# Convolution and experts of a one-layer trunk: the inverse's last step respread over groups, and two matmuls of the expert projections merged into one

## The chip, the cores and the metric

The kernel runs on one core of a Trainium2 chip. The metric is device time in microseconds (us). The engines are TensorE (PE for matmuls, PEld for its weight loads), VectorE (DVE), ScalarE (ACT), GpSimd (POOL) and SyncE (SP); each works through its own queue in order. Transfers are issued by SP, POOL and ACT and carried by 16 shared DMA engines.

## The reference, cut to what matters

One layer over 2048 tokens of width 1024: adaLN, a Hyena mixer, a residual norm, and a mixture of 16 experts, each of which takes the 256 tokens that score highest for it.

```python
v, x1, x2 = jnp.split(u, 3, -1)                    # u: input projection and a 3-tap convolution
def long_conv(zin, o):
    y = irfft(rfft(zin, n=2 * L) * kf[o], n=2 * L)[:L]
    return y + zin * f_bias[o]
z = x1 * long_conv(v, 0)
z = x2 * long_conv(z, 1)
...
he = silu(xe @ w1) * (xe @ w3)                      # xe: the 256 tokens of an expert
ye = (he @ w2) * gate                               # added into the tokens' rows
```

All is float32. Where the kernel wants more speed than a float32 matmul it writes a number as a sum of two fp32r parts, high and low, and sums three products: high·high, high·low, low·high. `mm3` (lines 174 to 177) issues these three.

## The kernel before, in words

**Convolution** (`phase_conv`, about 1037 to 1606 us of the trace). The FFT is done as matmuls in steps. There are 8 jobs (`jobs`): four blocks of 256 channels for the first long convolution (jobs 0 to 3), then four for the second (4 to 7). A job has 16 groups `gp`, so the loop over `order` has 128 turns. What a turn does is written out by hand, and the order in the code is the order on every engine. A turn of group n holds:

- `fetch_k` and `fetch`: every second turn, 512 KB of filter spectra (`kr`) and of signal (`xr`), issued on SP up to nine turns ahead;
- `spec`, three turns ahead: two float32 matmuls on the filter into a bank `xp`, and four half-height ACT copies from it into `k`, the last one (line 832) with the sign turned;
- `fwd`, two turns ahead: two matmuls on the signal into `xp`, then four DVE operations that make the complex product `pz`;
- `inv`: two matmuls from `pz` into the one bank `ap`, an ACT copy into one of three tiles `ao`, and one turn later (`LAG`) two POOL-issued transfers of 128 KB that scatter `ao` into `bn` (`put`). An `ao` is free again when its transfers have landed.

When a job's 16 groups lie in `bn`, the inverse's last step takes eight pieces q, during the next job: `bst` (at gp 2 to 9, one a turn) multiplies a piece of `bn` into a bank `sb`; one turn later `gate` multiplies by `x` on DVE. In the first convolution `bsplit` first makes high and low parts of pieces 3 to 7 (two ACT casts, two POOL subtractions, one turn ahead), `gate` also splits its result (one ACT cast, one POOL subtraction), and `s1st` (at gp 4 to 11) starts the next convolution's forward step: for each of two halves th three fp32r matmuls of 512 columns into `sb`, an ACT copy into `s1t`, a POOL-issued store to `z1d`. In the second convolution `gate`'s result is stored to `zd` from POOL. `fetch_x` loads `x` two pieces at a time at gp 0, 2, 4, 6. The eight PSUM banks are four `xp`, three `sb`, one `ap`.

**Experts** (`phase_moe`, about 1915 to 4170 us). Per expert there are 16 turns (8 slices `fc` of the hidden width, 2 halves i). `project` writes one bank `ab` of two halves of 256 columns, one for w1 and one for w3: for each of them eight k-steps of `mm3` with 256 token columns. `flush` then issues the previous turn's `back`: 12 fp32r matmuls of 512 columns into four banks `acc`. `hidden` is a chain ACT silu, DVE product (line 1487), ACT cast `hh`, DVE subtraction `hl`; its result is read by `back` one turn later. Besides, each slice's weights are split (line 1380 an ACT cast, line 1381 a DVE subtraction, 128x2048 each, three times a slice), and `route` gathers and transposes the next expert's tokens into `xh` and `xl`, through two banks `tp`. For the first 13 experts a planner orders the instructions from its own cost estimates, in the order of the code where several are ready; the last three experts have an order written by hand.

Of the kernel before, what the change touches and what calls it, by code (L numbers as in the profile page):

```python
# [12 lines left out]
F32 = mybir.dt.float32  # L13
# [756 lines left out]
def phase_conv(tc, A, wst, s2, am, fud, ud, x1d, x2d, z1d, zd, O, after):  # L770
# [5 lines left out]
    with ExitStack() as st:  # L776
# [21 lines left out]

        def s1st(j, q):
            zh, zl = zs.pop((j, q))  # L800
            for th in range(2):
                p = ps.tile([128, 2, 256], F32, name="sb", bufs=3)
                mm3(nc, p, s1h[:, th], s1l[:, th], zh, zl)
                t = rt.tile([128, 2, 256], F32, name="s1t", bufs=3)
                nc.scalar.copy(t, p)
                nc.gpsimd.dma_start(z1d[jobs[j][0], th].rearrange("g (s n) c -> (g s) n c", s=8)[:, 2 * q:2 * q + 2], t)

# [14 lines left out]
        def spec(j, gp):  # L822

            r = kr.pop((j, gp))
            p = ps.tile([128, 2, 256], F32, name="xp", bufs=4)
            for i in range(2):
                nc.tensor.matmul(p[:, i], lhsT=s2[:, 2 * gp + i], rhs=r[:, i], start=True, stop=True)  # L827
            k = rt.tile([128, 2, 2, 256], F32, name="k", bufs=3)
            nc.scalar.copy(k[0:64, 0], p[0:64])
            nc.scalar.copy(k[64:128, 0], p[0:64])  # L830
            nc.scalar.copy(k[64:128, 1], p[64:128])
            nc.scalar.activation(k[0:64, 1], p[64:128], AF.Copy, scale=-1.0)
            if gp == 0:
                nc.vector.tensor_copy(k[64:65, 0, 0], k[64:65, 1, 0])
                nc.vector.memset(k[0:1, 1, 0], 0.0)
                nc.vector.memset(k[64:65, 1, 0], 0.0)
            kk[j, gp] = k
# [3 lines left out]
        def fwd(j, gp):  # L841
# [15 lines left out]
        def inv(j, gp):  # L857
# [8 lines left out]
            ao = wk.tile([128, 2, 256], F32, name="ao", bufs=3)  # L866
            nc.scalar.copy(ao, p)
# [31 lines left out]
        def bst(j, q):  # L899
            p = ps.tile([128, 2, 256], F32, name="sb", bufs=3)  # L900
            if jobs[j][1] == 0:
# [13 lines left out]
        def gate(j, q, p):  # L915
# [18 lines left out]
        order = [(j, gp) for j in range(8) for gp in range(16)]  # L934

        def ahead(n):
# [7 lines left out]
        for n, (j, gp) in enumerate(order):  # L944
            if j > 0 and gp % 2 == 0 and 0 <= gp < 8:
                fetch_x(j - 1, gp - 0)
            while bps:
                gate(*bps.pop(0))
            ahead(n)
            if 4 <= gp < 9 and j > 0:  # L950
                bsplit(j - 1, gp - 1)
            if 2 <= gp < 10 and j > 0:
                bst(j - 1, gp - 2)
            q = gp - 4
            if (j + 3, q) in zs:
                s1st(j + 3, q)
            inv(j, gp)
# [27 lines left out]
        def first(q):  # L985
            tag = ("xp", "sb")[q % 2] if q < 7 else "ap"
            halves.append(ps.tile([128, 2, 256], F32, name=tag, bufs={"xp": 4, "sb": 3, "ap": 1}[tag]))
            nc.tensor.matmul(halves[q], lhsT=zero[:, 0:128], rhs=zero, start=True, stop=False)
            last(q, 0)
# [430 lines left out]
def phase_moe(tc, A, rowd, ident, ones_f, lg, R, xnd, accd, out):  # L1420
    nc = tc.nc
    tab, lo, hi, slot, spf = R.tab, R.lo, R.hi, R.slot, R.spf
    with ExitStack() as st:
# [7 lines left out]
        def route(e):  # L1431
# [4 lines left out]
            yield  # L1436
            p = ps.tile([128, 2, 33], F32, name="tp")
            idx = wk.tile([128, 2], I32, name="idx", bufs=4)
# [15 lines left out]
            yield  # L1454
            xh = wk.tile([128, 8, 256], F32R, name="xh")
            xl = wk.tile([128, 8, 256], F32R, name="xl")
            nxt[:] = [idx, gate, xh, xl]
            for q in range(4):
                p = ps.tile([128, 2, 256], F32, name="tp")
# [4 lines left out]
                nc.scalar.copy(xh[:, 2 * q:2 * q + 2], p)  # L1464
                nc.vector.tensor_tensor(xl[:, 2 * q:2 * q + 2], p, f_(xh[:, 2 * q:2 * q + 2]), OP.subtract)
                yield
# [6 lines left out]

        def project(i, x, ws):

            xh, xl = x
            fs = slice(i * 128, i * 128 + 128)
            p = ps.tile([128, 2, 256], F32, name="ab")
            for j in range(2):
                for k in range(8):  # L1480
                    mm3(nc, p[:, j], ws[2 * j][:, k, fs], ws[2 * j + 1][:, k, fs], xh[:, k], xl[:, k], start=(k == 0), stop=(k == 7))
            return p

        def hidden(p):
            s = wk.tile([128, 256], F32, name="s")
            nc.scalar.activation(s, p[:, 0], AF.Silu)  # L1486
            nc.vector.tensor_tensor(s, s, p[:, 1], OP.mult)  # L1487
            hh = wk.tile([128, 256], F32R, name="hh")
# [22 lines left out]

        def settle(name, idx=None):


            x = wk.tile([128, 2, 1024], F32, name=name)
            if idx is None:
# [48 lines left out]
        for e in range(NE - 3):  # L1565
            idx, gate, *x = nxt
            acc = [[pa.tile([128, 512], F32, name=f"acc{h}{q}") for q in range(2)] for h in range(2)]
# [18 lines left out]
        with tc.manual_schedule():  # L1586
# [4 lines left out]
            for e in range(NE - 3, NE):  # L1591
                prev = acc, idx, gate
                idx, gate, *x = nxt
                acc = [[pa.tile([128, 512], F32, name=f"acc{h}{q}") for q in range(2)] for h in range(2)]
                rt = iter(()) if e == NE - 1 else route(e + 1)
                for n in range(16):
                    fc, i = divmod(n, 2)
                    if i == 0:
                        ws, nw = nw, []
                    p = project(i, x, ws)  # L1600
                    flush()
# [14 lines left out]
                    if todo:  # L1616
                        act.append(settle(todo[-2:], prev[1] if todo[0] == "-" else None))
                        next(act[-1])
# [10 lines left out]
            flush()  # L1629
            ys = [wk.tile([128, 1024], F32, name=n) for n in ("xh", "xl")]  # L1630

# [131 lines left out]
```

## Time and profile before

| | |
|---|---|
| time, median of 3 runs | 4176.95 us (4176.51 to 4177.35) |
| the profiled execution: its own time, and its span | 4177.93 us, 4176.1 us |
| mean granted TensorE clock | 0.971 |
| busy: PE, PEld, DVE, ACT, POOL | 93%, 80%, 63%, 45%, 26% of the span |
| DMA | 832.14 MB, 199 GB/s mean |

The span runs from the first to the last instruction; the execution has 1.8 us around it. Busy shares are means over stages with different limits, so the rows below are taken per stage. A matmul's duration in the trace is longer than the distance to the next one, because matmuls are pipelined; what one costs is the distance between starts.

### The profile page before, as it was taken

How to read it: one execution, taken by the hardware profiler on the slowest of the kernel's cores; microseconds unless marked ns; L12 is line 12 of the kernel's file. 1: busy time of each engine (PE TensorE's matmuls, PEld its weight loads, DVE VectorE, ACT ScalarE, POOL GpSimd, SP SyncE). 2: the span in 40 equal slices, each digit the busy share in tenths (PEclk: the TensorE clock that was granted, in tenths of full speed). 3: DMA queues.
4: the chain of work that ended last, by engine and by line, in shares of the span. 5: the costliest groups of instructions: out<-in, count | busy, mean ns of one | idle time of the engine just before them, and what ended most of it. 6: DMA issues, size and time to landing. Idle time of an engine off the chain costs nothing.

```text
span 4176.1 us, 59155 instructions
## 1 busy us (share of the span) xinstructions
PE 3898.9 (93%) x23158; PEld 3350.6 (80%) x23158; DVE 2639.2 (63%) x3636; ACT 1885.7 (45%) x2609; POOL 1067.4 (26%) x1106
## 2 busy tenths in 40 slices
PE   6788999999989998956999999999999999999997
PEld 2445787877767786746999999999999999998996
DVE  6997454776877786885555555555555555556666
ACT  4554332333888772122444444444444444444443
POOL 4674221221566542130000000000000000005635
PEclk7999999999999999977999999999999999999999
DMA  6565355666998996453656665666566656656664
GB/s 190 184 210 177 119 163 170 204 205 207 256 257 230 262 281 204 162 176 108 202 193 210 192 202 193 208 193 203 192 208 193 203 193 203 200 170 226 231 229 166
DMA packets 645843, 832.14 MB, mean 199 GB/s; under 512 B 56883, under 2 KB 532803, under 8 KB 643260
## 3 DMA queue, kind: packets, MB, share of 16 engines
q1 hardware_dynamic: 576066, 678.56, 50.9%
q0 software_dynamic: 52512, 146.97, 12.1%
q10 hardware_dynamic: 16986, 2.83, 0.4%
q8 instruction: 182, 2.98, 0.3%
q14 instruction: 97, 0.79, 0.1%
HBM read 643.82 MB, written 150.75 MB: 190 GB/s over the span
## 4 chain that ended last, share of the span: by engine, by line
PE 74%; DVE 8%; DMA 7%; POOL 4%; issue 3%; ACT 2%; SPq 0%; ACTq 0%; POOLq 0%; DVEq 0%
PE ab L175 11%; PE ab L177 11%; PE ab L176 11%; PE acc L175 5%; PE acc L176 5%; PE acc L177 5%; PE ip L175 4%; PE ip L177 4%; PE ip L176 4%; DMA bn<-ao 4%; PE op L175 1%; PE op L177 1%; PE op L176 1%; PE xp L827 1%; PE ap L865 1%
## 5 line engine op out<-in xcount | busy, mean ns | idle before, releaser
L177 PE MATMUL ab<-xh,w1l 128*128 128x256 f32 x2048 | 581.4, 284 | 3.1 <-DVE w1l L1381 2.9
L175 PE MATMUL ab<-xh,w1h 128*128 128x256 f32 x2048 | 582.8, 285 | 0.0
L177 PE MATMUL ab<-xh,w3l 128*128 128x256 f32 x2048 | 579.7, 283 | 0.5 <-DVE w3l L1381 0.5
L176 PE MATMUL ab<-xl,w1h 128*128 128x256 f32 x2048 | 579.8, 283 | 0.0
L176 PE MATMUL ab<-xl,w3h 128*128 128x256 f32 x2048 | 579.6, 283 | 0.0
L175 PE MATMUL ab<-xh,w3h 128*128 128x256 f32 x2048 | 579.6, 283 | 0.0
L1381 DVE TENSOR_TENSOR w2l<-w2r,w2h 128x2048 fp32r<-128x2048 f32 x126 | 297.5, 2361 | 316.9 <-ACT w2h L1380 316.9
L175 PE MATMUL acc<-w2h,hh 128*128 128x512 f32 x1024 | 404.3, 395 | 13.4 <-ACT hh L170 13.4
L176 PE MATMUL acc<-w2l,hh 128*128 128x512 f32 x1024 | 402.7, 393 | 0.0
L177 PE MATMUL acc<-w2h,hl 128*128 128x512 f32 x1024 | 400.1, 391 | 0.8 <-DVE hl L171 0.8
L175 PEld LDWEIGHTS ab<-xh,w1h 128*128 128x128 f32 x2048 | 392.5, 192 | 8.9 <-ACT xh L1464 0.3
L176 PEld LDWEIGHTS ab<-xl,w1h 128*128 128x128 f32 x2048 | 392.5, 192 | 8.6
L177 PEld LDWEIGHTS ab<-xh,w1l 128*128 128x128 f32 x2048 | 392.2, 192 | 4.1 <-DVE w1l L1381 4.1
L177 PEld LDWEIGHTS ab<-xh,w3l 128*128 128x128 f32 x2048 | 393.2, 192 | 0.9 <-DVE w3l L1381 0.9
L176 PEld LDWEIGHTS ab<-xl,w3h 128*128 128x128 f32 x2048 | 393.2, 192 | 0.0
L175 PEld LDWEIGHTS ab<-xh,w3h 128*128 128x128 f32 x2048 | 393.2, 192 | 0.0
L1487 DVE TENSOR_TENSOR s<-s,ab 128x256 f32<-128x256 f32 x256 | 106.8, 417 | 399.5 <-ACT s L1486 399.5
L1510 POOL DMA_INDIRECT accd<-y,idx x27 | 64.4, 2385 | 1117.5 <-DVE y L1504 1117.5
L1381 DVE TENSOR_TENSOR w1l<-w1r,w1h 128x2048 fp32r<-128x2048 f32 x126 | 300.9, 2388 | 69.6 <-ACT w1h L1380 69.4
L1381 DVE TENSOR_TENSOR w3l<-w3r,w3h 128x2048 fp32r<-128x2048 f32 x126 | 292.9, 2325 | 53.8 <-ACT w3h L1380 53.8
L1380 ACT CAST w2h<-w2r 128x2048 fp32r<-128x2048 f32 x128 | 244.0, 1906 | 152.2 <-PE acc L177 144.3
L1486 ACT ACTIVATE s<-ab 128x256 f32<-128x256 f32 x256 | 97.4, 380 | 446.0 <-PE ab L177 446.0
(402 smaller groups left out, 8822.5 us busy)
## 6 DMA issues: line engine op xcount, KB each, us to landing
w1r<-in_moe_w_dram SPq DMA_DIRECT2D x128, 1024.0 KB
w3r<-in_moe_w_dram SPq DMA_DIRECT2D x128, 1024.0 KB
w2r<-in_moe_w_dram SPq DMA_DIRECT2D x128, 1024.0 KB
fud<-ev SPq DMA_DIRECT2D x128, 256.0 KB
kr<-fud SPq DMA_DIRECT2D x64, 512.0 KB
bn<-ao POOLq DMA_DIRECT2D x248, 128.0 KB, 7.2
mw<-in_mod_w_dram SPq DMA_DIRECT2D x96, 256.0 KB
wraw<-in_hy_w_in_dram SPq DMA_DIRECT2D x48, 512.0 KB
```

The lines of the kernel that those rows point to most:

```text
L175: nc.tensor.matmul(out, lhsT=ah, rhs=bh, start=start, stop=False)
L176: nc.tensor.matmul(out, lhsT=ah, rhs=bl, start=False, stop=False)
L177: nc.tensor.matmul(out, lhsT=al, rhs=bh, start=False, stop=stop)
L827: nc.tensor.matmul(p[:, i], lhsT=s2[:, 2 * gp + i], rhs=r[:, i], start=True, stop=True)
L865: nc.tensor.matmul(p[:, i], lhsT=am[:, 2 * gp + i], rhs=z[:, i], start=True, stop=True)
L1380: nc.scalar.copy(h, raw)
L1381: eng.tensor_tensor(l, raw, f_(h), OP.subtract)
L1486: nc.scalar.activation(s, p[:, 0], AF.Silu)
L1487: nc.vector.tensor_tensor(s, s, p[:, 1], OP.mult)
L1510: nc.gpsimd.indirect_dma_start(out=accd, out_offset=at(idx, h), in_=y, in_offset=None, compute_op=OP.add)
```

## The change

In the convolution: pieces go to gp 3, 5, 6, 8, 10, 12, 13 and 15 of the next job (for the last job gp 3 to 10); `s1st` does one half th a turn, from a list `todo`; `ap` has two banks and `sb` two; `ao` cycles through seven tiles, four of them new; the sign-turned fourth copy of `k` is gone, and DVE does one half of the product without the sign. In experts 1 to 13: high and low token parts lie side by side in one tile `xs`, and one matmul of 512 columns takes both; the two sums are put in the two halves of a bank, one bank for w1 and one for w3, and are added afterwards (an ACT copy and a DVE addition each). `ab` has three banks, `tp` one. The last three experts keep the three matmuls (`project_summed`, the old order), reading `xs`; their `settle` steps use halves of a tile `xs` where they used tiles `xh` and `xl`.

```diff
-        def s1st(j, q):
-            zh, zl = zs.pop((j, q))
-            for th in range(2):
-                p = ps.tile([128, 2, 256], F32, name="sb", bufs=3)
+        def s1st(j, q, th):
+            zh, zl = zs[j, q]
+            p = ps.tile([128, 2, 256], F32, name="sb", bufs=2)
...
-            nc.scalar.activation(k[0:64, 1], p[64:128], AF.Copy, scale=-1.0)
...
-            for h in range(2):
-                a, b = slice(64 * h, 64 * h + 64), slice(64 - 64 * h, 128 - 64 * h)
-                nc.vector.scalar_tensor_tensor(q[a], p[b], -1.0, k2[b], op0=OP.mult, op1=OP.mult)
+            nc.vector.scalar_tensor_tensor(q[0:64], p[64:128], -1.0, k2[64:128], op0=OP.mult, op1=OP.mult)
+            nc.vector.tensor_tensor(q[64:128], p[0:64], k2[64:128], OP.mult)
...
-            p = ps.tile([128, 2, 256], F32, name="ap", bufs=1)
+            p = ps.tile([128, 2, 256], F32, name="ap", bufs=2)
...
+            m = j * 16 + gp
+            if m % 7 < 4 and m < 122:
+                ao = rt.tile([128, 2, 256], F32, name="ao2", bufs=4)
+            else:
+                ao = wk.tile([128, 2, 256], F32, name="ao", bufs=3)
...
+                todo.extend((j + 4, q, th) for th in range(2))
...
+            at = (3, 5, 6, 8, 10, 12, 13, 15) if j < 7 else range(3, 11)
+            return at.index(gp) if j > 0 and gp in at else None
...
-            if j > 0 and gp % 2 == 0 and 0 <= gp < 8:
-                fetch_x(j - 1, gp - 0)
+            ready = todo[:1]
+            q = q_at(j, gp + 1)
+            if q is not None and q % 2 == 0:
+                fetch_x(j - 1, q)
             while bps:
                 gate(*bps.pop(0))
             ahead(n)
-            if 4 <= gp < 9 and j > 0:
-                bsplit(j - 1, gp - 1)
-            if 2 <= gp < 10 and j > 0:
-                bst(j - 1, gp - 2)
-            q = gp - 4
-            if (j + 3, q) in zs:
-                s1st(j + 3, q)
+            if q is not None and q > 2:
+                bsplit(j - 1, q)
+            q = q_at(j, gp)
+            if q is not None:
+                bst(j - 1, q)
+            if ready:
+                s1st(*todo.pop(0))
             inv(j, gp)
...
+            for j in range(2):
+                p = ps.tile([128, 2, 256], F32, name="ab", bufs=3)
+                for k in range(8):
+                    nc.tensor.matmul(p, lhsT=ws[2 * j][:, k, fs], rhs=xs[:, k], start=(k == 0), stop=False)
+                    nc.tensor.matmul(p[:, 0], lhsT=ws[2 * j + 1][:, k, fs], rhs=xs[:, k, 0], start=False, stop=(k == 7))
+                u = wk.tile([128, 256], F32, name=f"u{j}", bufs=2 - j)
+                nc.scalar.copy(u, p[:, 1])
+                nc.vector.tensor_tensor(u, p[:, 0], u, OP.add)
+                if j == 0:
+                    nc.scalar.activation(u, u, AF.Silu)
```

## Rows read from the trace of the kernel before

**Rows 1.** The page: the chain that ended last, share by engine.
```profile
PE 74%; DVE 8%; DMA 7%; POOL 4%; issue 3%; ACT 2%; SPq 0%; ACTq 0%; POOLq 0%; DVEq 0%
```
**Rows 2.** Stretches: length, busy PE, PEld, DVE, ACT, POOL, clock, DMA share, GB/s.
```profile
1041.00:1093.00 52.00, 47.97 (x202) 36.98 (x203) 47.79 (x72) 47.36 (x86) 20.22 (x34) 1.00 1.10 269
1093.00:1405.90 312.90, 276.22 (x1134) 213.34 (x1132) 222.75 (x307) 253.61 (x461) 206.76 (x266) 0.98 0.89 247
1405.90:1530.10 124.20, 117.64 (x641) 101.74 (x641) 98.62 (x149) 90.34 (x158) 50.79 (x81) 0.99 1.00 266
1530.10:1585.40 55.30, 46.47 (x267) 40.74 (x267) 38.08 (x57) 33.15 (x57) 23.12 (x37) 0.95 1.00 286
2500.00:3000.00 500.00, 500.00 (x3544) 471.04 (x3543) 266.31 (x276) 215.47 (x215) 23.06 (x14) 1.00 0.61 198
```
**Rows 3.** Chain of waits, 1037 to 1607 us: by line; pieces (start, us).
```profile
by line: DMA bn<-ao 26.2%; PE ap L865 9.1%; PE xp L827 8.3%; issue 7.9%; PE sb L911 7.8%; PE xp L847 7.3%; DMA z1d<-s1t 3.9%; DMA a<-in_c_ra_dram 3.5%; POOL bn L874 3.4%; PE sb L904 3.2%; ACT ao L867 3.0%; POOL z1d L806 2.5%; PE sb L175 2.0
...
1100.19 1.72 PE sb L904 x4
...
1429.42 1.78 PE sb L911 x16
1431.20 0.87 PE ap L865 x4
```
**Rows 4.** Waits, 1037 to 1607 us: waiter, releaser, total us, times, longest.
```profile
PEld ap L865 <- ACT ao L867: 49.3, 50, 7.6
PE ap L865 <- ACT ao L867: 29.7, 29, 7.2
ACT ao L867 <- DMA bn<-ao: 29.4, 29, 7.8
```
**Rows 5.** Groups by line and form, 1041 to 1585 us (busy, mean ns).
```profile
L852 DVE SCALAR_TENSOR_TENSOR qz<-xp,k 64x512 f32<-64x512 f32 x251 | 172.8, 688 | 99.3 <-PE xp L847 91.2 <-ACT s1t L805 3.5 <-ACT ao L867 1.0
...
L854 DVE TENSOR_TENSOR pz<-pz,qz 128x512 f32<-128x512 f32 x126 | 106.2, 843 | 4.3
...
L867 ACT COPY ao<-ap 128x512 f32<-128x512 f32 x127 | 74.9, 590 | 78.9 <-DMA bn<-ao 29.4 <-issue 22.0 <-PE ap L865 20.9
L832 ACT ACTIVATE k<-xp 64x512 f32<-64x512 f32 x124 | 73.7, 595 | 2.9
...
L896 POOL TENSOR_TENSOR w<-bn,w 128x512 fp32r<-128x512 f32 x40 | 50.6, 1284 | 10.7 <-ACT w L895 10.6
```
**Rows 6.** DMA packets, 1050 to 1070 us, then 1530 to 1560 us.
```profile
DMA packets 4302, 4.92 MB, mean 246 GB/s; under 512 B 704, under 2 KB 3908, under 8 KB 4300
...
DMA packets 6044, 9.48 MB, mean 316 GB/s; under 512 B 955, under 2 KB 4077, under 8 KB 6041
```
**Rows 7.** Landing of transfers from ao, issued 1050 to 1060, then 1096 to 1112.
```profile
DMA to landing us min/median/max: 7.8/8.0/8.1
...
DMA to landing us min/median/max: 3.7/4.0/4.1
```
**Rows 8.** TensorE's timeline in an expert: start, us, line, operation.
```profile
2505.27 0.28 PE L175 MATMUL ab<-xh,w1h 128*128 128x256 f32 x1
...
2511.02 0.40 PE L175 MATMUL acc<-w2h,hh 128*128 128x512 f32 x1
...
2513.77 0.28 PE L175 MATMUL ab<-xh,w1h 128*128 128x256 f32 x1
```
**Rows 9.** Timelines of ACT and DVE, 2501 to 2522 us.
```profile
2504.42 0.38 ACT L1486 ACTIVATE s<-ab 128x256 f32<-128x256 f32 x1
...
2504.55 2.29 DVE L1381 TENSOR_TENSOR w3l<-w3r,w3h 128x2048 fp32r<-128x2048 f32 x1 [0.59 <-ACT w3h L1380]
...
2507.64 0.43 DVE L171 TENSOR_TENSOR hl<-s,hh 128x256 fp32r<-128x256 f32 x1 [0.47 <-ACT hh L170]
```
**Rows 10.** Waits of TensorE's weight loads, 1915 to 4170 us.
```profile
PEld acc L175 <- DVE y L1504: 1.4, 5, 0.4
...
PEld tp L1463 <- DVE xl L1465: 0.2, 1, 0.2
```

More of the change, by code (lines that the diff above doesn't have):

```diff
@@ L797, in phase_conv @@
         zs = {}
-        def s1st(j, q):
-            zh, zl = zs.pop((j, q))
-            for th in range(2):
-                p = ps.tile([128, 2, 256], F32, name="sb", bufs=3)
[L803 to L806, printed above, removed]
+        def s1st(j, q, th):
+            zh, zl = zs[j, q]
+            p = ps.tile([128, 2, 256], F32, name="sb", bufs=2)
+            mm3(nc, p, s1h[:, th], s1l[:, th], zh, zl)
+            t = rt.tile([128, 2, 256], F32, name="s1t", bufs=3)
+            nc.scalar.copy(t, p)
+            nc.gpsimd.dma_start(z1d[jobs[j][0], th].rearrange("g (s n) c -> (g s) n c", s=8)[:, 2 * q:2 * q + 2], t)
         def fetch(j, gp):
@@ L899, in bst @@
         def bst(j, q):
-            p = ps.tile([128, 2, 256], F32, name="sb", bufs=3)
+            p = ps.tile([128, 2, 256], F32, name="sb", bufs=2)
             if jobs[j][1] == 0:
@@ L934, in phase_conv, with q_at @@
         order = [(j, gp) for j in range(8) for gp in range(16)]
+        todo = []
+        def q_at(j, gp):
+            at = (3, 5, 6, 8, 10, 12, 13, 15) if j < 7 else range(3, 11)
+            return at.index(gp) if j > 0 and gp in at else None
         def ahead(n):
@@ L985, in first @@
         def first(q):
-            tag = ("xp", "sb")[q % 2] if q < 7 else "ap"
-            halves.append(ps.tile([128, 2, 256], F32, name=tag, bufs={"xp": 4, "sb": 3, "ap": 1}[tag]))
+            tag = "xp" if q % 2 == 0 else "sb" if q < 4 else "ap"
+            halves.append(ps.tile([128, 2, 256], F32, name=tag, bufs={"xp": 4, "sb": 2, "ap": 2}[tag]))
             nc.tensor.matmul(halves[q], lhsT=zero[:, 0:128], rhs=zero, start=True, stop=False)
@@ L1436, in route @@
             yield
-            p = ps.tile([128, 2, 33], F32, name="tp")
+            p = ps.tile([128, 2, 33], F32, name="tp", bufs=1)
             idx = wk.tile([128, 2], I32, name="idx", bufs=4)
@@ L1454, in route @@
             yield
-            xh = wk.tile([128, 8, 256], F32R, name="xh")
-            xl = wk.tile([128, 8, 256], F32R, name="xl")
-            nxt[:] = [idx, gate, xh, xl]
+            xs = wk.tile([128, 8, 2, 256], F32R, name="xs")
+            nxt[:] = [idx, gate, xs]
             for q in range(4):
-                p = ps.tile([128, 2, 256], F32, name="tp")
+                p = ps.tile([128, 2, 256], F32, name="tp", bufs=1)
                 for i in range(2):
@@ L1463, in route @@
                         nc.tensor.transpose(out=p[:, i, h * 128:h * 128 + 128], in_=xg[h][:, k * 128:k * 128 + 128], identity=ident)
-                nc.scalar.copy(xh[:, 2 * q:2 * q + 2], p)
-                nc.vector.tensor_tensor(xl[:, 2 * q:2 * q + 2], p, f_(xh[:, 2 * q:2 * q + 2]), OP.subtract)
+                xh, xl = (xs[:, 2 * q:2 * q + 2, c] for c in range(2))
+                nc.scalar.copy(xh, p)
+                nc.vector.tensor_tensor(xl, p, f_(xh), OP.subtract)
                 yield
@@ L1510, in finish, with settle @@
                 nc.gpsimd.indirect_dma_start(out=accd, out_offset=at(idx, h), in_=y, in_offset=None, compute_op=OP.add)
-        def settle(name, idx=None):
-            x = wk.tile([128, 2, 1024], F32, name=name)
+        def settle(x, idx=None):
             if idx is None:
@@ L1565, in phase_moe @@
         for e in range(NE - 3):
-            idx, gate, *x = nxt
+            idx, gate, x = nxt
             acc = [[pa.tile([128, 512], F32, name=f"acc{h}{q}") for q in range(2)] for h in range(2)]
@@ L1592, in phase_moe @@
                 prev = acc, idx, gate
-                idx, gate, *x = nxt
+                idx, gate, x = nxt
+                free = wk.tile([128, 2, 2, 1024], F32, name="xs")
                 acc = [[pa.tile([128, 512], F32, name=f"acc{h}{q}") for q in range(2)] for h in range(2)]
@@ L1616, in phase_moe @@
                     if todo:
-                        act.append(settle(todo[-2:], prev[1] if todo[0] == "-" else None))
+                        act.append(settle(free[:, todo[-1] == "l"], prev[1] if todo[0] == "-" else None))
                         next(act[-1])
@@ L1629, in phase_moe @@
             flush()
-            ys = [wk.tile([128, 1024], F32, name=n) for n in ("xh", "xl")]
+            free = wk.tile([128, 2, 2, 1024], F32, name="xs")
+            ys = [free[:, h, 0] for h in range(2)]
             def newton(h):
```

25 lines of the change are left out of this document (14 added, 11 removed).

## The prediction

> **What bounds the kernel now.** I read the chain that ended last first: TensorE holds 74% of it, DVE 8%, DMA 7% [rows 1]. The two places of the change then need the busy times by stretch [rows 2]: in the experts (2500 to 3000) PE is busy for all 500 us at clock 1.00, DVE 266, ACT 215, and DMA moves 198 GB/s at a share of 0.61. There only cheaper matmuls help. In the convolution it is not so: in jobs 1 to 4 (1093 to 1405.9) PE is busy 276 of 312.9 us, by modelled ends, so its own work is less; no engine is full, and DMA has a share of 0.89 to 1.10.
>
> What the convolution waits for is in its own chain and waits [rows 3, 4]. The largest entry of the chain is no engine: the transfer from `ao` into `bn`, 26.2%. The mechanism is in the waits: the ACT copy into `ao` waited 29.4 us for a transfer out of that tile to land, and PE with its loads waited 29.7 + 49.3 = 79 us for that copy to free the single `ap` bank. With three tiles, three turns take one landing plus a copy and an issue. A landing took 8.0 us in the plain turns from 1050 to 1060, but 4.0 us in the first turns with a piece [rows 7].
>
> **The convolution, part by part.**
>
> PE's floor. A pair of float32 matmuls of 256 columns costs 0.87 us, and a turn has three pairs: 2.61 us, 41.8 a job. A piece costs 1.72 us in float32 in the first convolution, 1.78 in the second [rows 3]. An fp32r matmul of 512 columns is 0.229 us (2.75 us for 12) [rows 8], so a piece in six of them is 1.37 and a half of `s1st` 0.69. Jobs 1 to 4: 41.8 + 3 x 1.72 + 5 x 1.37 + 16 x 0.69 = 64.9, four times 259.6 us, against 312.9 now. The next two: 41.8 + 8 x 1.78 = 56.0, twice 112, against 124.2. The last stretch is PE's 46.5 busy of 55.3 [rows 2]. In job 0 the floor is DVE: three products at 0.688 and an addition at 0.843 [rows 5] are 2.91 us a turn, 46.5 a job, against 52.
>
> The other engines do not stand in the way on average. The sign-turned copy saves ACT 0.595 us a turn [rows 5], 38 us of its 253.6 in jobs 1 to 4; 216 remain, DVE's 223 and POOL's 207 are unchanged in amount [rows 2]. On DVE a product without the sign has the same shape as the one that it replaces, and I count no change. The removed copy is worth most in job 0, where ACT now has 47.4 busy of 52.0: it falls to 38, and DVE is late next.
>
> The seven `ao` tiles give a transfer seven turns to land, at 2.9 us or more a turn over 20 us, against the 8.0 measured: the wait for `ao` goes. The second `ap` bank lets PE start a turn before the copy is done: the 79 us go as far as something else is not later. What takes their place is, I think, partly TensorE's own work and partly transfers. The four stretches move 14.0 + 77.3 + 33.0 + 15.8 = 140.1 MB [rows 2]. Where all 16 engines were busy throughout, they moved 246 GB/s in plain turns and 316 in turns with pieces [rows 6]; 140.1 MB are 443 us at 316. Jobs 1 to 4 alone are 245 us at 316, and 291 at the 266 GB/s that jobs 5 and 6 have over their length. PE's 259.6 lies between them, so two queues of like load share the stretch.
>
> What is moved: each piece carries its `gate`, on DVE, its split (ACT, POOL) or store (POOL), and the `x` load on SP, now issued one turn ahead of the first of its two pieces instead of two. SP passes no transfer that it did not have before it; a load has two turns until `gate` reads it, and it is costed at nothing, hidden by those 6 to 8 us; without that cover DVE would stand a few us four times a job. The first piece needs the previous job's last `ao` in `bn`; at gp 3 instead of 2 it has a turn more, so it costs nothing where landings stay near 8 us. On POOL a turn before a piece now holds up to three splits of 1.284 us [rows 5] behind each other, 3.9 us, plus two or three issues; the second half of the next piece waits for the last of them. I put 0.4 us on each of 20 such pieces, 8 us in all, between 0 (POOL is busy two thirds now) and 20 x 1.284 = 26. `sb` loses a bank, but holds a half of `s1st` a turn instead of two; nothing, with the ACT copy of the turn before as its cover, and a copy's 0.59 us a turn if that is gone.
>
> Sum, with PE or DVE at the floor and a part of the difference given back to transfers and POOL: job 0 49 (between 46.5 and 52), jobs 1 to 4 280 (between 259.6 and 291), the next two 118 (between 112 and 124), the last stretch 52 (46.5 to 55.3). That is 499 against 544.4: 45 us less. Ends: 80 less with every floor reached, 22 less with jobs 1 to 4 at 266 GB/s and the rest as now.
>
> **The experts.** A turn is 48 matmuls of 256 columns in 5.75 us (2505.27 to 2511.02), 119.8 ns each, and 12 of 512 columns in 2.75 us, 229.2 ns each [rows 8]. At the 2.4 GHz level (clock 1.00), 256 columns are 106.7 ns and 512 are 213.3: each matmul, with its own weight load, costs 13 to 16 ns over its columns. Three of 256 columns, 359.4 ns, become one of 512 and one of 256, 349.0: 10.4 ns less, 16 times a turn, 0.166 us of 8.50. Times 16 turns and 13 experts: 34.5 us less. The ends: nothing if the wide one costs two narrow ones, and 13 ns more a step (another 44 us) if the narrow one, its load hidden by the wide one, falls to its columns. I take the rows' own prices, since both forms stand there side by side.
>
> The Trainium skill, TensorE: Matmul & The Clock Gate, section Back-to-back issue gap, gives for matmuls at the full clock a distance of the columns plus 2.5 ns. By that the merged pair would save 2.5 ns a step, 8 us in all by an estimate from the page. The rows disagree with it here: 119.8 and 229.2 ns are 13 and 16 over the columns, and each of these matmuls has a weight load before it.
>
> The two copies and two additions a turn (ACT about 0.38 each by the silu of the same shape, DVE about 0.42 by `hl` [rows 9]) bring ACT from 43 to 52% and DVE from 53 to 63%: hidden by PE's 8.33 us a turn. Slots are not late: with three `ab` banks a bank returns after another 5.5 us. Each expert's first `back` waits for the last weighing of the one before; PE and its loads now wait 1.4 us in all for that [rows 10], so they are level, and up to 0.17 us of the gain is waited away per expert, 2 us. I take 33 less.
>
> The last three experts keep their matmuls: nothing, by PE's unchanged order there; so does the tail.
>
> Sum: 4177.9 (the profiled execution) - 45 - 33 = 4100. The median of the runs is 1 us under that execution: **4099 us**.
>
> **Rivals.**
>
> 1. *Transfers take the wait over.* For it: shares of 1.00 to 1.10 in all stretches without `s1st` [rows 2], and landings double there. Against: 316 GB/s was reached. Then the convolution gives 22, and the time is 4122. Chance 0.20.
>
> 2. *Slower: the hidden activations come late.* `back` reads `hh` and `hl` of the turn before. At 2511.02 it starts; `hl` ended at 2508.07 [rows 8, 9]: 2.95 us of room, 2.78 with the shorter turn. The new addition takes 0.42; if one subtraction of 2.29 and one cast of 1.91 more get ahead of the chain on DVE and ACT, it is 4.6 longer, and PE waits 1.84 us. That meets the turn in which two weights are split, 8 an expert, 104 in all: 191 us, 4290. It decides from a chain 2.78 longer, and makes the kernel slower than before from 3.5 longer (78 / 104 = 0.75 us of wait). Against: DVE and ACT are idle a third and a half of a turn, and the first bank's sum is made 2.8 us earlier. Chance 0.06.
>
> 3. *The single `tp` bank.* Four quarters of the transposed tokens share it; each has a cast (0.59) and a subtraction (0.69) to wait for. In full that is 3 x 1.28 x 13 = 50 us, 4149. Against: the planner places other matmuls between, and the wait is now 0.2 us [rows 10]. Chance 0.06.
>
> 4. *Cost by column.* If 119.8 ns are the price of 256 columns of tokens whatever the instruction, the experts give nothing: 4132. Against: the 229.2 of the same kind of operand. The page's floor of 2.5 ns would be close to this, at 4124 by an estimate. Chance 0.08.
>
> 5. *Floors nearly reached.* Convolution 70 less, experts 33: 4074. For it: turns with pieces ran back to back on PE in the chain (1429.42 to 1432, no gap). Chance 0.12.
>
> **How the numbers follow.** The forecast has 0.48. Under 4062 would need every floor and a cheaper narrow matmul; over 4138 needs rival 2, 3, or 1 and 4 together: the range is 4062 to 4138, with about 0.05 and 0.12 outside. A measurement of this kernel can tell about 0.2%, 8 us, from no change. Slower by more than that is most of rival 2, 0.05; within it 0.03 (a mild rival 2 or several together); faster 0.92.
>
> **What would show it.** In the trace after: no wait of `ao` for its transfer, and of PE for `ao` under 15 us; jobs 1 to 4 in 260 to 291 us at 265 to 300 GB/s; a turn of an expert 8.33 us with `ab` at 5.58; PE busy throughout, and no new wait on `hh`. The prediction is wrong if expert turns are over 8.45, or if the convolution's stretch is as long as now with DMA shares near 1.1.

## The result: 4124.3 us, faster by 1.3%

The changed kernel takes 4124.33 us (median of 4 runs, 4120.1 to 4128.35), against 4177.15 for the kernel before in the same runs (4176.51 to 4179.38): a ratio of 0.9872, 95% interval 0.9855 to 0.989. The forecast was 4099, its range 4062 to 4138. The direction and the two places of the gain came out; the gain is 53 us where 78 were forecast, and the reason given for the convolution's part, more tiles and a second bank, accounts for a quarter of it at most by the runs below.

The profile after, in the order of the rows of before. The page's chain by engine, which answers to [rows 1]:

```profile
PE 73%; DVE 10%; issue 5%; POOL 5%; DMA 4%; ACT 2%; SPq 0%; ACTq 0%; POOLq 0%; DVEq 0%
```

Transfers fell from 7 to 4%, VectorE rose from 8 to 10%. The stretches that answer to [rows 2] (same columns; job 0, jobs 1 to 4, jobs 5 and 6, most of the last job):

```profile
1037.00:1084.00 47.00, 44.91 (x192) 34.70 (x191) 45.37 (x68) 36.79 (x64) 18.64 (x32) 1.00 1.11 278
1084.00:1371.00 287.00, 265.56 (x1121) 209.38 (x1120) 220.75 (x300) 218.11 (x390) 207.69 (x260) 1.00 0.89 262
1371.00:1490.00 119.00, 116.05 (x652) 105.29 (x651) 98.62 (x148) 76.39 (x132) 53.77 (x87) 0.99 1.08 292
1490.00:1550.00 60.00, 53.91 (x309) 46.93 (x307) 41.82 (x62) 27.95 (x49) 25.50 (x40) 0.97 0.99 285
```

Jobs 1 to 4 went from about 310 to 286 us. TensorE is closer to full (265.6 of 287), but 21 us of the stretch are still not its. The waits between 1037 and 1573, which answer to [rows 4]:

```profile
PEld sb L176 <- POOL w L896: 20.9, 22, 1.1
...
ACT ao L867 <- DMA bn<-ao: 11.8, 2, 6.9
PE sb L176 <- POOL w L896: 11.4, 22, 0.6
...
PE sb L175 <- DVE z L924: 9.5, 7, 1.5
...
PEld sb L175 <- DVE z L924: 7.0, 5, 1.8
...
PEld ap L861 <- ACT ao L867: 3.0, 1, 3.0
...
PE ap L861 <- ACT ao L867: 2.6, 1, 2.6
```

TensorE's 29.7 us of waits for `ao` and its loads' 49.3 are 2.6 and 3.0 now. (The prediction adds the first two to 79 us. They are mostly the same time seen twice: in the trace of before 29.6 us of them are idle on both, so some 49 us is all that there was.) ScalarE's wait for transfers is 11.8 us at two places, both in the last job. New at the head are waits for POOL's subtraction (L896, the low half of a split piece) and for VectorE's gate (L924), which frees an `sb` bank.

The starts of ScalarE's copies into `ao` (one a group) give the length of each job; the last one runs to its last copy. The two columns at the right are runs told of below.

| job | before | after | as after, ao and banks of before | three edits |
|---|---|---|---|---|
| 0 | 49.6 | 47.3 | 49.1 | 46.7 |
| 1 | 75.2 | 70.8 | 72.7 | 72.9 |
| 2 | 75.8 | 72.2 | 71.8 | 68.8 |
| 3 | 81.1 | 71.0 | 71.0 | 70.0 |
| 4 | 77.7 | 72.2 | 75.2 | 68.8 |
| 5 | 62.3 | 59.7 | 61.2 | 59.0 |
| 6 | 61.5 | 59.7 | 56.5 | 57.0 |
| 7 | 61.7 | 63.4 | 66.1 | 64.6 |

Before to after: job 0 -2.3, jobs 1 to 4 -23.6, jobs 5 and 6 -4.4, job 7 +1.7, together -28.6. The first copy comes 4.8 us earlier as well, at 1035.69 against 1040.53, but that is not the change's doing: in the run with the experts' edits alone, whose convolution is as before, it comes at 1034.10. Traces with the same convolution differ by up to 3 us over the eight jobs (544.9 and 547.5 with the old one, 515.2 to 517.6 in three with the new one).

In the experts, TensorE's timeline answers to [rows 8] (start, us, line, operation): the `ab` block of a turn runs from 2508.31 to 2513.95.

```profile
2508.31 0.39 PE L1491 MATMUL ab<-xs,w1h 128*128 128x512 f32 x1
2508.54 0.28 PE L1492 MATMUL ab<-xs,w1l 128*128 128x256 f32 x1
2508.65 0.40 PE L1491 MATMUL ab<-xs,w1h 128*128 128x512 f32 x1
...
2513.95 0.40 PE L175 MATMUL acc<-w2h,hh 128*128 128x512 f32 x1
```

That is 5.64 us for 16 pairs, 352.5 ns a pair, where three narrow ones took 359.4. POOL's timeline shows each expert's first scatter of its result; the first and the eleventh of a series ten experts long:

```profile
2030.50 1.62 POOL L1537 DMA_INDIRECT accd<-y,idx  x1 [71.99 <-DVE y L1531]
...
3396.64 1.61 POOL L1537 DMA_INDIRECT accd<-y,idx  x1 [72.01 <-DVE y L1531]
```

136.61 us an expert; in the trace of before the same two stand at 2064.36 and 3447.78, 138.34 an expert. 1.73 x 13 = 22.5 us.

### The profile page after: what moved, and what is told of

Its sections match the earlier page's. It is cut to its first block, busy times and chain, and to the rows that moved or that the text cites. A ratio compares the mean times of both kernels' runs of the same rounds, so it can differ in the third digit from the quotient of the medians.

```text
span 4122.7 us, 53152 instructions
## 1 busy us (share of the span) xinstructions
PE 3857.8 (94%) x19830; PEld 3163.6 (77%) x19830; DVE 2798.6 (68%) x4044; ACT 1959.5 (48%) x2897; POOL 1077.3 (26%) x1106
## 3 DMA queue, kind: packets, MB, share of 16 engines
q0 software_dynamic: 52512, 146.97, 12.2%
## 4 chain that ended last, share of the span: by engine, by line
PE 73%; DVE 10%; issue 5%; POOL 5%; DMA 4%; ACT 2%; SPq 0%; ACTq 0%; POOLq 0%; DVEq 0%
PE ab L1491 19%; PE ab L1492 10%; PE acc L175 5%; PE acc L176 5%; PE acc L177 5%; PE ip L175 4%; PE ip L177 4%; PE ip L176 4%; PE op L175 1%; PE op L177 1%; PE op L176 1%; PE sp L336 1%; PE ab L177 1%; PE ab L176 1%; PE ab L175 1%
## 5 line engine op out<-in xcount | busy, mean ns | idle before, releaser
L1491 PE MATMUL ab<-xs,w3h 128*128 128x512 f32 x1664 | 600.4, 399 | 0.0
L1491 PE MATMUL ab<-xs,w1h 128*128 128x512 f32 x1664 | 598.0, 399 | 0.0
L1492 PE MATMUL ab<-xs,w3l 128*128 128x256 f32 x1664 | 468.2, 281 | 0.0
L1492 PE MATMUL ab<-xs,w1l 128*128 128x256 f32 x1664 | 466.5, 280 | 0.0
L175 PE MATMUL acc<-w2h,hh 128*128 128x512 f32 x1024 | 404.2, 395 | 14.5 <-ACT hh L170 13.8
L1491 PEld LDWEIGHTS ab<-xs,w3h 128*128 128x128 f32 x1664 | 313.0, 188 | 76.4
L1491 PEld LDWEIGHTS ab<-xs,w1h 128*128 128x128 f32 x1664 | 313.0, 188 | 72.8
L1492 PEld LDWEIGHTS ab<-xs,w1l 128*128 128x128 f32 x1664 | 314.2, 189 | 7.1
L1492 PEld LDWEIGHTS ab<-xs,w3l 128*128 128x128 f32 x1664 | 314.8, 189 | 0.0
L1389 ACT CAST w1h<-w1r 128x2048 fp32r<-128x2048 f32 x128 | 244.5, 1910 | 80.2 <-PE ab L1491 79.0
L1389 ACT CAST w3h<-w3r 128x2048 fp32r<-128x2048 f32 x128 | 244.6, 1911 | 68.3 <-PE ab L1491 66.2
```

What stands on the lines that cost most here:

```text
L175: nc.tensor.matmul(out, lhsT=ah, rhs=bh, start=start, stop=False)
L1389: nc.scalar.copy(h, raw)
L1491: nc.tensor.matmul(p, lhsT=ws[2 * j][:, k, fs], rhs=xs[:, k], start=(k == 0), stop=False)
L1492: nc.tensor.matmul(p[:, 0], lhsT=ws[2 * j + 1][:, k, fs], rhs=xs[:, k, 0], start=False, stop=(k == 7))
```

## The experiments

All are timed against the kernel before on the same chip; ratios have 95% intervals. The kernel after is at 0.9872 (0.9855 to 0.989), so two of them have to differ by some 0.0024 (10 us) before the time alone tells them apart; below that the traces decide.

| run | us | ratio to before | interval |
|---|---|---|---|
| convolution alone | 4149.35 | 0.9924 | 0.991 to 0.9938 |
| experts alone | 4152.16 | 0.9932 | 0.9918 to 0.9946 |
| wide matmuls grouped | 4112.11 | 0.9832 | 0.9818 to 0.9846 |
| pieces 0, 1, 6 unsplit | 4122.35 | 0.9853 | 0.9836 to 0.9871 |
| split first | 4134.26 | 0.9898 | 0.9882 to 0.9914 |
| row written by ScalarE | 4115.48 | 0.9848 | 0.9834 to 0.9862 |
| stores on SP | 4127.87 | 0.9884 | 0.9868 to 0.99 |
| three ao tiles | 4124.66 | 0.9873 | 0.9857 to 0.9888 |
| one ap bank | 4127.72 | 0.9873 | 0.9856 to 0.989 |
| three ao tiles, one ap bank | 4130.24 | 0.988 | 0.9864 to 0.9897 |
| three edits | 4099.62 | 0.9804 | 0.9788 to 0.982 |
| three edits, split first | 4097.94 | 0.9804 | 0.9787 to 0.9821 |

**The two halves.** Each run has one half's part of the diff and the other half as before. At the core, against after, the first has

```diff
-                    nc.tensor.matmul(p, lhsT=ws[2 * j][:, k, fs], rhs=xs[:, k], start=(k == 0), stop=False)
-                    nc.tensor.matmul(p[:, 0], lhsT=ws[2 * j + 1][:, k, fs], rhs=xs[:, k, 0], start=False, stop=(k == 7))
+                    mm3(nc, p[:, j], ws[2 * j][:, k, fs], ws[2 * j + 1][:, k, fs], xh[:, k], xl[:, k], start=(k == 0), stop=(k == 7))
```

and the second

```diff
-            at = (3, 5, 6, 8, 10, 12, 13, 15) if j < 7 else range(3, 11)
...
+            if 2 <= gp < 10 and j > 0:
+                bst(j - 1, gp - 2)
```

> The edits of the convolution alone, experts as before. Theory: the two halves don't touch, and the landmarks of the two traces hold: the stage after the convolution starts 33.1 us earlier, so 4177.2 - 33 = 4144 us (4141 to 4147). Rival, the split of the prediction (45 of the convolution, 33 of the experts): 4132 us. If the halves help each other (weights of the first experts loaded while the convolution runs), this and the run of the experts alone together give less than the 52.8 us of both.

> The edits of the experts alone, convolution as before. Theory: 1.73 us less per expert between two scatters, times 13 = 22.5, of which the end of the trace kept 20.3: 4177.2 - 20 = 4157 us (4154 to 4159). Rival, the prediction's own 33: 4144 us.

Measured against 4178.67: 29.3 us and 26.5 us, 55.8 together, against 52.8 for the whole change. They add up within the spread, so each can be studied alone. The theory's split (33 and 20) is off by a few us each way; some 5 us of its 33 were the earlier start told of above. The prediction's 45 lies outside the convolution's interval (26 to 38 us). Its 33 lies inside the experts' (23 to 34 us); there it is the scatters (22.5) that speak against it.

**The price of a wide and a narrow matmul.**

```diff
                 for k in range(8):
                     nc.tensor.matmul(p, lhsT=ws[2 * j][:, k, fs], rhs=xs[:, k], start=(k == 0), stop=False)
+                for k in range(8):
                     nc.tensor.matmul(p[:, 0], lhsT=ws[2 * j + 1][:, k, fs], rhs=xs[:, k, 0], start=False, stop=(k == 7))
```

> As after, but the eight wide matmuls of a projection first and then its eight narrow ones, instead of one wide and one narrow in turn; same matmuls. Theory A (a matmul costs by its columns, 236 for 512 and 117 for 256, whoever its neighbour is): pair stays at 352.5 ns, time within 3 us of after, 4121 to 4128 us. Theory B (the change between the two shapes costs): a pair nearer 346 ns, 3328 pairs x 6.5 ns = 21 us less, 4103 us. Theory C (a wide matmul hides the weight load of the narrow one behind it, two narrow ones in a row go back to 119.8 each as before): pair 356 to 358 ns, 3328 x 4 = 12 us more, 4137 us.

Theory B, at some six tenths of its size. TensorE's timeline of this run (x8: eight in a row):

```profile
2513.16 1.98 PE L1491 MATMUL ab<-xs,w1h 128*128 128x512 f32 x8
2514.97 1.11 PE L1493 MATMUL ab<-xs,w1l 128*128 128x256 f32 x8
2515.92 2.00 PE L1491 MATMUL ab<-xs,w3h 128*128 128x512 f32 x8
2517.76 1.12 PE L1493 MATMUL ab<-xs,w3l 128*128 128x256 f32 x8
2518.71 0.40 PE L175 MATMUL acc<-w2h,hh 128*128 128x512 f32 x1
```

Eight wide ones take 1.81 and 1.84 us (226 and 230 ns each), eight narrow ones 0.95 (119 ns each), and the block is 5.55 us. The median block between 2460 and 2600 is 5.56, the prediction's 5.58 nearly to the digit. So [rows 8] gave the right prices, for matmuls among their like. In turn, a pair costs 352.5 instead of 347.5 ns. What in the alternation costs the 5 ns is not told apart: with the width, the high and the low weights alternate too. POOL's scatters come every 135.54 us here: 1.07 x 13 = 13.9 us less than after, and 12.2 were measured.

**Which of the convolution's edits brought the gain.** Three kernels undo the tiles, the bank, and both; the spreading and the copy that is left out stay.

```diff
-            if m % 7 < 4 and m < 122:
+            if False:
```

> As after, with the three ao tiles of before instead of seven; everything else of the change stays. Theory of the prediction (with three tiles ScalarE's copy waits for the transfer two groups back, and TensorE for the copy): most of the convolution's gain of 29 goes, 4124 + 20 = 4144 us (4136 to 4152), and ScalarE waits for bn<-ao again, 30 us or more between 1030 and 1570. Rival: spreading the last step has by itself lowered the rate to 263 GB/s, at which a transfer lands in time; the four tiles are worth under 6 us: 4124 to 4130 us.

```diff
-            p = ps.tile([128, 2, 256], F32, name="ap", bufs=2)
+            p = ps.tile([128, 2, 256], F32, name="ap", bufs=1)
...
-            p = ps.tile([128, 2, 256], F32, name="sb", bufs=2)
+            p = ps.tile([128, 2, 256], F32, name="sb", bufs=3)
```

> As after, with one ap bank and three sb banks, as before, and the seven ao tiles kept. With three ao tiles and two banks ScalarE waited 75.2 us for transfers and the time stayed, so the tiles are not what brought the convolution's 29 us. Theory: the second ap bank is: with one, each inverse waits for ScalarE's copy of the group before, as in the 59.8 us of waits (PE 20.9, its loads 38.9) before: 4124 + 15 = 4139 us (4132 to 4150). Rival: the spreading and the copy that is left out brought it, and either the tiles or the bank is cover enough: 4121 to 4128 us, TensorE's waits for ScalarE's ao under 10 us.

> As after, with three ao tiles and one ap bank (three sb), as before: of the change to the convolution only the spreading and the copy that is left out remain. Theory (the second bank brought most of it, the tiles nothing): as with one bank alone, 4139 us, at most 5 us more. Rival 1 (tiles and bank each cover for the other): the run with one bank is at 4124 and this one at 4145 us or above. Rival 2 (spreading and copy brought all): 4121 to 4130 us.

The first fell to its rival at 0.9873, the same as after. The waits of that run, 1037 to 1573:

```profile
ACT ao L867 <- DMA bn<-ao: 75.2, 44, 8.7
...
PEld ap L861 <- ACT ao L867: 3.9, 2, 3.7
...
PE ap L861 <- ACT ao L867: 3.3, 1, 3.3
```

ScalarE waits 75.2 us for the transfers, more than twice the 29.4 of [rows 4], and no time is lost: with a second `ap` bank TensorE waits 3.3 us for it. My next theory, that the bank then did it, fell as well: with one bank and seven tiles the ratio is again 0.9873. With neither, ScalarE's waits are larger than before, and TensorE's and its loads' are back in part, at 21.0 and 26.5 us against 29.7 and 49.3:

```profile
ACT ao L867 <- DMA bn<-ao: 72.9, 48, 8.3
...
PEld ap L861 <- ACT ao L867: 26.5, 12, 7.5
...
PE ap L861 <- ACT ao L867: 21.0, 10, 6.8
```

and the ratio is 0.988, at most a few us over after. Of these waits little lies where the gain is. What TensorE waited for in jobs 1 to 4, in before (1090 to 1400 us) and then in the run with neither (1087 to 1378):

```profile
PE ap L865 <- ACT ao L867: 14.9, 15, 2.5
PE sb L904 <- DMA bn<-ao: 7.7, 4, 2.2
PE sb L175 <- DVE z L924: 6.6, 4, 1.7
PE sb L176 <- POOL w L896: 4.5, 10, 1.9
```

```profile
PE sb L176 <- POOL w L896: 12.4, 20, 0.9
PE sb L175 <- ACT w L895: 6.3, 4, 2.6
PE ap L861 <- ACT ao L867: 1.4, 2, 1.1
```

So in these jobs TensorE's waits for `ao` are gone (14.9 us, now 1.4) with the tiles and the bank of before; the 21.0 us lie mostly in the last job (14.2) and in job 0 (3.8). Gone too are the 7.7 us for which each job's first piece waited for the transfers of the job before. Rival 2 it is, in the main: spreading the last step and leaving out the copy bring jobs 1 to 4 from 309.8 to 290.7 us by themselves, 19.1 of the 23.6, and all eight jobs from 544.9 to 523.6, 21.3 of the 28.6. The rest in jobs 1 to 4 goes with the banks and not with the tiles: they take 290.6 us with one `ap` bank and seven tiles, 284.9 with two banks and three. The tiles are worth something in job 0, which has no last step beside it: it takes 49.3 and 49.1 us with three tiles, 47.3 with seven, be it one bank or two. Two things were not tried: how the 19 us divide between the spreading and the copy (in job 0, without the tiles, the copy left out brings at most 0.5 us in these two traces, 49.6 to 49.1), and what tiles and bank would have brought with the last step left where it was.

**What the stretch waits for now.** In the middle of jobs 1 to 4 of after two groups take 8.8 us, and groups 12 and 13 take 6.4 and 7.1 (in jobs 1, 2 and 4). The timeline of after, all engines, shows the second case (the bracket is the idle time before and what ended it):

```profile
1203.81 3.85 DVE L850 TENSOR_TENSOR pz<-pz,qz 128x512 f32<-128x512 f32 x1
...
1204.60 2.51 POOL L896 TENSOR_TENSOR w<-bn,w 128x512 fp32r<-128x512 f32 x2
...
1208.41 0.47 PE L175 MATMUL sb<-w,bmh 128*128 128x512 f32 x1 [1.52 <-DVE z L924]
...
1210.62 0.28 DVE L832 COPY k<-k 1x256 f32<-1x256 f32 x1 [2.36 <-ACT k L830]
...
1214.78 0.50 PE L175 MATMUL sb<-w,s1h 128*128 128x512 f32 x1 [1.44 <-DVE z L924]
```

Two things make VectorE's gate late here, and TensorE with it: an addition that takes 3.85 us while POOL subtracts twice, and a one-row copy (L832, once a job) for which VectorE stands 2.36 us behind ScalarE's queue. Four runs take these apart.

```diff
-                    if q < 3:
+                    if q in (0, 1, 6):
...
-            if q is not None and q > 2:
+            if q is not None and q not in (0, 1, 6):
                 bsplit(j - 1, q)
```

> As after, but of the eight pieces of a job 0, 1 and 6 go unsplit instead of 0, 1 and 2: the two pieces that lie one group apart (groups 5 and 6, 12 and 13) are then never both split ones; the number of split pieces stays five. Theory: POOL's four subtractions in a row at groups 11 and 12 hold VectorE and with it the product of the next piece, 6.4 and 7.1 us for two groups where their neighbours take 4.4, so some 4 us a job go in jobs 1 to 4: 4124 - 16 = 4108 us (4106 to 4114), with these two groups at 4.4 to 5. Rival: the jobs are bound by their transfers or by TensorE's floor and the time comes back elsewhere in the job: 4121 to 4128 us.

The rival, as far as the time can tell (2 us). Group 12 moved as the theory says, group 13 by less than half of it, and most of the gain was lost next door: job 2 has 5.0, 6.2 and 5.6 from group 12 on, where after has 6.4, 7.1 and 4.0. What was left is the one-row copy:

```diff
-                nc.vector.tensor_copy(k[64:65, 0, 0], k[64:65, 1, 0])
-                nc.vector.memset(k[64:65, 1, 0], 0.0)
+                nc.scalar.copy(k[64:65, 0, 0], p[64:65, 0])
+                nc.scalar.activation(k[64:65, 1, 0], p[64:65, 0], AF.Copy, scale=0.0)
```

> As after, but the one row of a job's first group that the inverse needs at another place is written by ScalarE straight from PSUM, not by VectorE behind ScalarE's copies. Theory: VectorE stands 2.4 us at this copy (1210.62 in the trace of after), so that its products and the gate behind it are late and TensorE stands 1.44 us for the gate at 1214.78; once a job, seven jobs: 1 to 2 us each, 4124 - 10 = 4114 us (4110 to 4120). Rival: what is late there is VectorE's addition of 3.85 us beside POOL's subtractions, and the copy only stands in the same place: 4121 to 4128 us.

Theory, to 1.5 us in the medians (the intervals of this run and of after still touch; the trace decides). Group 13 falls from 7.1 to 4.4 us in jobs 1, 2 and 4; ScalarE pays 0.36 and 0.37 us for the row, and VectorE's next addition starts at 1209.18, in after at 1213.43. The addition ahead of it still takes 3.83 us, so the rival, which held it to be the cause at this place, falls:

```profile
1202.60 3.83 DVE L850 TENSOR_TENSOR pz<-pz,qz 128x512 f32<-128x512 f32 x1
...
1209.18 0.69 DVE L850 TENSOR_TENSOR pz<-pz,qz 128x512 f32<-128x512 f32 x1
...
1209.26 0.36 ACT L832 COPY k<-xp 1x256 f32<-1x256 f32 x1
...
1209.53 0.37 ACT L833 ACTIVATE k<-xp 1x256 f32<-1x256 f32 x1
```

For the middle, is POOL full, or only started late?

```diff
-            nc.gpsimd.dma_start(z1d[jobs[j][0], th].rearrange("g (s n) c -> (g s) n c", s=8)[:, 2 * q:2 * q + 2], t)
+            nc.sync.dma_start(z1d[jobs[j][0], th].rearrange("g (s n) c -> (g s) n c", s=8)[:, 2 * q:2 * q + 2], t)
```

> As after, but the stores of the last step of the forward part (one a group) are issued by SP instead of POOL: POOL sheds 0.6 us a group, 64 in all. Theory (POOL full in order bounds the middle of jobs 1 to 4 at 8.85 us for two groups): POOL's own work falls to 6.7 of these, TensorE's waits for POOL (11.4 us) mostly go: 4124 - 10 = 4114 us (4106 to 4119). Rival 1 (POOL is not full, the subtraction only starts late behind ScalarE): 4121 to 4128 us. Rival 2: SP waits for ScalarE's copy at each store and its loads behind it come late: over 4130 us, with waits of TensorE for the loads.

```diff
+            if q is not None and q > 2:
+                bsplit(j - 1, q)
             while bps:
                 gate(*bps.pop(0))
             ahead(n)
-            if q is not None and q > 2:
-                bsplit(j - 1, q)
```

> As after, but in each group the two halves of a piece are split before the gate and before the group's own work instead of behind them: ScalarE rounds and POOL subtracts some 2 us earlier. Theory: in the middle of jobs 1 to 4 TensorE stands 0.6 us per split piece for POOL's second subtraction (22 waits, 11.4 us), and that wait goes: 4124 - 10 = 4114 us (4108 to 4119), two groups in 8.2 to 8.4 us instead of 8.85. Rival: POOL is full in order (two subtractions 2.98, one 1.29, six DMA issues 3.6, so 7.9 of 8.85 us), the split then waits behind POOL's other work and the time stays: 4121 to 4128 us.

It is not full: with the stores off POOL, TensorE waits 10.9 us for it in 20 waits, as before, and no time is won. It starts late: with the split ahead of the gate four groups in the middle of job 2 take 16.3 us instead of 17.6, as that theory said. But the whole run is slower, which neither theory had: at the end of each job the earlier subtractions fall beside an addition (all engines, this run):

```profile
1211.28 3.11 DVE L850 TENSOR_TENSOR pz<-pz,qz 128x512 f32<-128x512 f32 x1
...
1211.35 2.48 POOL L896 TENSOR_TENSOR w<-bn,w 128x512 fp32r<-128x512 f32 x2
...
1214.32 0.68 DVE L924 TENSOR_TENSOR z<-sb,x 128x512 f32<-128x512 f32 x1
...
1215.05 0.79 PE L175 MATMUL sb<-w,s1h 128*128 128x512 f32 x1 [3.85 <-DVE z L924]
```

and that group takes 10.0 us. Over the convolution 22 of its 125 additions are lengthened, by 37.1 us in all over the usual 0.69 (counting those over 0.75 us); in after it is 15, by 19.8.

**A version that beats both.**

> Three edits together: the eight wide matmuls before the eight narrow ones, the row of a job's first group written by ScalarE, pieces 0, 1 and 6 unsplit. Alone they measured 12.2, 8.9 and 2 us less than after, 23.1 together: 4101 us (4097 to 4105). Theory: the third was worth little alone because VectorE's wait for that row took its place at the next group (6.2 us for a group in its trace), so with the row gone its two groups fall from 6.4 and 4.4 to 4.7 and 4.4 too, 1.7 x 4 = 7 us more: 4094 us (4089 to 4098). Rival: the sum, 4101 us.

> As the run with the three edits, and pieces 2 to 5 split ahead of the gate, piece 7 as after. Theory: alone and for all pieces this took four groups in the middle from 17.6 to 16.3 us and lost 10 us where the split of the last piece put POOL's subtractions beside VectorE's addition; without that piece the gain stays, 1.3 to 2 us a job: 5 to 8 us under the run with the three edits. Rival: POOL's subtractions then meet the additions of other groups (2.1 to 2.3 us for one in that trace) and the time is the same or up to 8 us more.

The second has, against the first:

```diff
+            if q in (2, 3, 4, 5):
+                bsplit(j - 1, q)
             while bps:
                 gate(*bps.pop(0))
             ahead(n)
-            if q is not None and q not in (0, 1, 6):
+            if q == 7:
                 bsplit(j - 1, q)
```

The three edits give 4099.62 us, ratio 0.9804 (0.9788 to 0.982), some 25 us under after. That is the rival's sum of the parts (4101) to 1.4 us and outside the theory's range (4089 to 4098). The trace has the theory's groups, nearly, 5.0 and 4.4 for 6.4 and 4.4 (jobs 2 and 4 at 68.8 us), and loses the gain at group 3 of job 1 (9.6 us against 7.9 in the run with the row alone): jobs 1 to 4 take 280.5 us, 281.0 with the row alone. So it is not shown that the third edit adds anything to the other two. With the split first in the middle, jobs 2 and 4 take 66.3 us, 1.4 over TensorE's floor of 64.9, and TensorE's waits for POOL fall from 11.4 to 2.5 us; but job 3 takes 72.1, and the ratio is the same. (In the traces the eight jobs are 6.2 us shorter, 501.6 against 507.8, the medians differ by 1.7: a small gain is neither shown nor excluded.) The timeline of job 3:

```profile
1257.72 3.93 DVE L850 TENSOR_TENSOR pz<-pz,qz 128x512 f32<-128x512 f32 x1
...
1262.30 0.70 PE L175 MATMUL sb<-w,s1h 128*128 128x512 f32 x1 [4.27 <-DVE z L924]
```

The same encounter, at another group. So the version with three edits stands: it beats both kernels. Of the 14.4 us that TensorE is idle in its jobs 1 to 4, 11.4 are waits for POOL's second subtraction; with the split first it is 10.0, and 4.9 of them are two waits for the gate, one of them the 4.27 behind the long addition above. How much the additions are lengthened in all does not decide: 13.9 us with the three edits, 27.9 with the split first, at times that can't be told apart.

## Why the prediction came out, and where it did not

**Experts, 33 forecast, 22.5 by the scatters, 26.5 alone.** The step that was too large is the term 349.0 ns for a wide matmul and a narrow one. Its two prices were read from blocks in which each shape stands among its like. They hold there (347.5 in the grouped run); in turn the pair costs 352.5. That is 3.5 ns more than forecast, x 16 x 16 x 13 = 11.6 us, which is nearly all that the scatters miss. The distance that the Trainium skill gives, TensorE: Matmul & The Clock Gate, section Back-to-back issue gap (the columns plus 2.5 ns), would have merging save 2.5 ns a pair; the runs show 6.9 in turn and 11.9 grouped. Everything else of this part held: TensorE is busy 500 of 500 us, ScalarE's and VectorE's new work is hidden (257 and 318 of 500 us), TensorE waits 13.8 us for `hh`, all of it in the last three experts as before, so rival 2 (hidden activations late) did not come. The single `tp` bank costs its loads 5.1 us in 26 waits, a tenth of rival 3.

**Convolution, 45 forecast, 29.3 alone.** By parts, measured against forecast: job 0 2.3 us for 3, jobs 1 to 4 23.6 for 33, the next two 4.4 for 6, and the last job none for 3. Three steps:

- *"The seven `ao` tiles give a transfer seven turns to land ...: the wait for `ao` goes"* and *"The second `ap` bank lets PE start a turn before the copy is done: the 79 us go"*. As events both came. As causes they account for a quarter of the gain at most (7.3 of 28.6 us): in jobs 1 to 4 TensorE's waits for `ao` go from 14.9 to 1.4 us without them, and 19.1 of the 23.6 us come without them. To the spreading, which with the copy left out brought these, the prediction gave no gain, only costs; of the first piece it says "it costs nothing", and moving it took away 7.7 us of waits. That the convolution's gain still fell inside the range is luck in that part. The size was misread too, since 79 counts TensorE and its loads for the same time. Whether those waits set the length of before, or only collected slack, stays open, as tiles and bank were not run without the spreading.
- *Jobs 1 to 4 at 280.* They take 286.2. I charged 8 us for POOL's late splits, and TensorE does wait 11.4 us for them, 4.5 before. Not in the sum were the gate behind a long addition and the one-row copy; removing that copy alone gave 9 us, 5.3 of them in these jobs. The additions of before have a median of 692 ns and a longest of 4084; I took their mean of 843 in [rows 5] for a price. In job 0, which has no split pieces, 0.692 makes the floor 44.1 us, not 46.5. The lengthening is not what the change took away: over the usual 0.69 us it is 19.0 us in before and 19.8 in after, at 15 additions each.
- *"`sb` loses a bank ... nothing"*. Its cover was ScalarE's copy; the bank is in fact freed by VectorE's gate too, and that is where TensorE's other 9.5 us are. With three `sb` banks and one `ap` bank these waits go and others come (8.3 us for ScalarE's split), and jobs 1 to 4 are 4 us longer.

Job 7 was forecast 3 shorter and is not: 63.4 to 64.8 us in three traces of the new convolution, 61.7 and 63.3 in two of the old. Its pieces lie a group later than before; whether that is the cause was not tried. Of the signs named, three missed by a little: 262 GB/s in jobs 1 to 4 where 265 to 300 were named, an `ab` block of 5.64 us where 5.58, and so a turn of 8.39 where 8.33.

**Rival 1** (transfers) gave 4122, close to the result, and is wrong: with ScalarE's waits for transfers at 75.2 us the time is the same, and the DMA share in jobs 1 to 4 is 0.89 in both traces. **Rival 4** (cost by column) is wrong too: grouped, 512 columns cost 226 to 230 ns and not twice 119.8. What no rival had is the alternation, which takes four tenths (5.0 of 11.9 ns) of what merging can give.

## What to carry to other kernels

A wait that leads the chain does not say which edit takes it away: here moving work to other turns, with a copy left out, did what the added buffers were meant to do. Undo the parts of a change one by one, and look in the stretch where the gain is. A wait that shows on TensorE and on its loads is counted once. A mean well above its median (843 and 692 ns here) is no price. A price read from a block of equal matmuls held for such blocks; in turn it was 5 ns a pair more. The one-row fix-up cost what stood ahead of it in its engine's order, not its 0.3 us.

## What the runs showed of the chip that I had not expected

**VectorE's addition and POOL.** The addition, with both inputs in SBUF, is lengthened at times; the product ahead of it, with one input in PSUM, never, though 24 of the products lie beside a subtraction of POOL as well. Durations (min, median, max in ns) of the product, then of the addition, in after:

```profile
L849 DVE TENSOR_TENSOR pz<-xp,k x125: 690/692/693, 1041.4 to 1540.9; 128x512 f32<-128x512 f32 x125
```

```profile
L850 DVE TENSOR_TENSOR pz<-pz,qz x125: 691/692/3851, 1042.2 to 1541.7; 128x512 f32<-128x512 f32 x125
```

All 15 long ones lie beside a subtraction of POOL, while a subtraction itself stays between 1.25 and 1.75 us. The Trainium skill, SBUF — State Buffer, section SBUF: two separate sides, names a port pair that is locked for a whole instruction, by a VectorE instruction with two SBUF inputs or by a GpSimd one that reads SBUF, whichever starts first. The trace agrees on who is hit. On who wins it differs, as far as recorded starts can tell: at 1203.81 the addition is recorded 0.8 us before POOL's subtractions and still ends only 0.55 us after both of them. POOL was issuing two transfers when it started (1203.37 to 1204.58), and these may have a part: in before three of its 15 long additions (1.56 to 1.76 us) lie beside transfers that POOL issues and beside no subtraction. But 72 additions of after lie so too and take their 0.69 us, so that part stays open.

**Alternating shapes.** A matmul of 512 columns and one of 256, each with its own weight load, cost 347.5 ns a pair in blocks of eight and 352.5 in turn, at a clock of 1.00 in both runs.
